# Two transformer blocks on one core: inputs turned by the host, weights in one array, and twelve idle matmuls at the start

## The chip, the core and the metric

The kernel runs on one core of one Trainium2 chip. The metric is device time in microseconds (us). Three runs of the kernel before gave 2495.00, 2495.05 and 2495.88 us; the median is 2495.05 us. The core's engines are called PE (TensorE, matrix products), ACT (ScalarE), DVE (VectorE), POOL (GpSimd) and SP (SyncE, which here only issues DMAs).

## The reference

256 tokens of 2048 features go through two blocks, all in float32. The first block has two layers; in each of them

```python
h = rmsnorm(x, norm_g[l])
proj = h @ w_in[l]                      # [256, 2048] @ [2048, 7168]
a_x, a_b, a_c, a_g, d_q, d_k, d_v, d_g, m_q, m_g = jnp.split(proj, offsets, axis=-1)
# a gated convolution over tokens (a_*), differential attention over the tokens (d_*)
mn = rmsnorm(mem, mem_norm_g[l])
mkv = mn @ w_mem_kv[l]                  # keys and values of 256 stored tokens, for the queries m_q
y = jnp.concatenate([y_a, y_d, y_m], axis=-1) @ w_out[l]
x = x + y
```

The second block projects again (`w_in_2`), runs two attention branches, merges them (`w_out_2`), attends to a second memory `mem_2` (normed, then `w_mem_kv_2`), and ends with a feed-forward part 2048 to 8192 to 2048 (`w_ff1_2`, `w_ff2_2`) and a last norm. A norm is `x * rsqrt(mean(x * x) + eps) * g`, over the features of one token. All weight matrices together are 440 MB and are used once.

## The kernel before

**Products.** Nearly all work is in `product`: 256 tokens times 512 columns of a weight matrix, over 16 feature tiles of 128. The activation lies "K-layout", features on the partitions, in tiles called A0h to A3h and B0h to B3h (high parts) and A0l to B3l (low parts), four feature tiles each, held in two slots "A" and "B"; the second index letter stands for high or low. Every float32 value is split into a part that the tensor engine's short format holds exactly (high) and the rest (low), and a product is three matmuls: high by high, high by low, low by high. The weights come in pieces of two feature tiles, 128 partitions by 1024 values (512 KB). For each piece SP issues a DMA into `raw` (L168, four buffers), ACT rounds it to `hi` (L169), DVE subtracts to get `lo` (L170, three buffers of hi and lo), and PE runs 12 matmuls (L187 hi by xh, L188 lo by xh, L189 hi by xl, for two feature tiles and two token tiles). In the listing's order `acc<-hi,A0h`, `hi` is the operand that streams through PE and `A0h` the one that is loaded into it. Eight pieces make a product.

**Work between the pieces.** After each piece `pump` runs one step of the background work (attention, the memory's preparation) and the delayed steps that are due; a scheduler then sets the order of the instructions on each engine under the limits that `issue_after` gives. Each engine runs its instructions in that order, so an ACT step that stands ahead of the next `hi` delays that `hi`.

**x and the memories.** Tensors arrive with tokens on the partitions. `first_input` loads x in four parts of 512 features in the first product, turns each by 8 transposes on PE (`to_klayout`, L156), and splits them from PSUM with the gains (L146 on ACT, L147 on DVE); ACT also squares the token-major x for the norm (L207). The gains are loaded by 18 small DMAs and turned by PE (L64, L392, L393). `memory_parts` does the same for `mem` in layer 0 and again in layer 1 (tile `mem_l`) and for `mem_2` (tile `mem_b`): four parts, each loaded, squared, turned by 8 transposes, split. A norm's factor 1/rms comes from `rsqrt`, some 17 small DVE steps (L85 to L87 are in it).

**The end.** The last product's weights (`last_weights`) are kept whole: pieces 0 to 3 in the tiles of slot A, pieces 4 to 7 in own tiles w4h to w7l, so that the two token tiles can be done one after the other (L966 to L968).

**Where tiles lie.** In a partition's memory the pools follow each other in the order in which they are opened: first the constants (`cst`), then slots A and B (`klp`), `raw` (`wrp`), `hi` and `lo` (`wsp`), and the rest; each tile takes a multiple of 32 bytes. In the built program the byte addresses are: A0h 39424, B0h 72192, `raw` from 104960, `hi` 121344, 125440 and 129536, `lo` from 133632, all of them multiples of 512; w4h is at 188096, w4l at 192192, and w4h to w7l are all 64 bytes past a multiple of 128. Of the attention's float32 tiles that stream through PE, `mv` is at 200384 (64 past a multiple of 128) and `pT` at 145920 and 147968 (multiples of 128).

Of the kernel before, what the change touches and what calls it, by code (L numbers as in the profile page):

```python
# [23 lines left out]
PSUM = bass.MemoryType.PSUM  # L24


@with_exitstack
def tile_two_blocks(
    ctx: ExitStack, tc: tile.TileContext,
    x, mem, norm_g, w_in, conv_w, conv_b, diff_q_norm_g, diff_k_norm_g, lambda_q1, lambda_k1,  # L30
    lambda_q2, lambda_k2, diff_head_norm_g, mem_norm_g, w_mem_kv, mem_q_norm_g, mem_k_norm_g,
    w_out, mem_2, positions_2, g_mix_2, w_in_2, g_cq_2, w_uq_2, w_iq_2, w_dsa_o_2, w_moba_o_2,
    w_out_2, g_mem_q_2, g_mem_kv_2, w_mem_q_2, w_mem_kv_2, w_mem_o_2, g_ff_2, w_ff1_2, w_ff2_2,
    g_final_2, out,
):
    nc = tc.nc
# [86 lines left out]
    class KLayout:  # L123
        """An activation with its features on the partitions, in two parts, in groups of four tiles."""
# [14 lines left out]
    def split(dst, src, gain=None):  # L139
        """dst = (hi, lo), each rounded to the tensor engine's short format; hi + lo = src * gain."""  # L140
# [8 lines left out]
    def to_klayout(kl, k0, nk, src, gain0=None):  # L149
        """Tiles k0.. of kl from src(t, j), [128 tokens, 128 features] each."""  # L150
# [14 lines left out]
    def weights(src, k0, nk, c0, n, hl=None):  # L165
        raw = wrp.tile([P, 2, 512], F32, name="raw", tag="raw")
        hi, lo = hl or [wsp.tile([P, 2, 512], F32R, name=a, tag=a) for a in ("hi", "lo")]
        nc.sync.dma_start(raw[:, 0:nk, 0:n], rows(src, k0 * P, nk * P, c0, n))  # L168
        A.activation(hi[:, 0:nk, 0:n], raw[:, 0:nk, 0:n], AF.Copy)  # L169
        V.tensor_tensor(lo[:, 0:nk, 0:n], raw[:, 0:nk, 0:n], hi[:, 0:nk, 0:n].bitcast(F32),  # L170
                        op=ALU.subtract)
# [181 lines left out]
    def first_input(i):  # L353
# [660 lines left out]
```

## Time and profile before

| | us |
|---|---|
| median of three runs | 2495.05 |
| the profiled execution, first to last instruction (span) | 2491.6 |
| median less span (the page gives no other time for the profiled execution) | 3.45 |
| PE busy | 2464.8 (99%) |
| DVE busy | 1423.0 (57%) |
| ACT busy | 1256.6 (50%) |
| PE idle between its instructions, all waits of the list by releaser | about 15 |

The span is the time from the first to the last instruction; what lies around it is the same launch work in every run and is not in the trace. PE's busy time counts a matmul from its start to a modelled end, so that neighbours overlap; the distance between the starts of two matmuls is what each costs. "Idle before" and the releaser behind "<-" tell what an engine waited for.

### The profile page before, as it was taken

To read this page: it belongs to the slowest core of one execution; us is meant where nothing else is said; L and a number is where in the kernel's file an instruction comes from. 1 tells how busy PE (TensorE), PEld (TensorE's weight loads), DVE (VectorE), ACT (ScalarE), POOL (GpSimd) and SP (SyncE) were. 2 spreads that over 40 slices of the span, in tenths; PEclk is the share of its full clock that TensorE was granted. 3 is DMA by queue.
4 is the path that set the end of the run, shared out by engine and by line. 5 is a ranking of instruction groups with operands and counts; after the bars stand their busy time and mean duration, and the time that the engine had idled before them with its cause. 6 is when DMAs were issued, how large, how long until landed. Compare 5 with 4: busy or idle time off the path is not lost.

```text
span 2491.6 us, 30607 instructions
## 1 busy us (share of the span) xinstructions
PE 2464.8 (99%) x11453; PEld 2035.2 (82%) x11453; DVE 1423.0 (57%) x2140; ACT 1256.6 (50%) x1808; POOL 3.3 (0%) x49
## 2 busy tenths in 40 slices
PE   8999999999999999999999999999999999999998
PEld 6888888888888888987888888888888888888876
DVE  6655566575556765555655545565645445445463
ACT  6554555465445554554554444565553443443452
POOL 0000000000000000000000000000000000000000
PEclk9999999999999999999999999999999999999999
DMA  6565555566655556654655566554665666666672
GB/s 229 183 186 165 173 162 183 185 206 187 180 168 167 170 182 177 192 171 136 195 174 163 173 190 194 179 192 156 184 186 193 188 190 192 190 187 194 186 243 87
DMA packets 234884, 450.76 MB, mean 181 GB/s; under 512 B 14260, under 2 KB 21104, under 8 KB 234608
## 3 DMA queue, kind: packets, MB, share of 16 engines
q1 hardware_dynamic: 234304, 446.72, 59.2%
q8 instruction: 90, 1.47, 0.2%
q10 hardware_dynamic: 432, 2.10, 0.2%
q14 instruction: 58, 0.48, 0.1%
HBM read 446.66 MB, written 2.10 MB: 180 GB/s over the span
## 4 chain that ended last, share of the span: by engine, by line
PE 95%; DMA 2%; ACT 2%; DVE 1%; issue 0%; SPq 0%; ACTq 0%; DVEq 0%
PE acc L187 29%; PE acc L189 29%; PE acc L188 29%; PE tr L156 2%; DMA mem_l<-in_mem_dram 1%; PE tr L294 1%; DMA raw<-in_w_ff_dram 1%; ACT hi L169 1%; PE sc L759 1%; PE sc L538 1%; DVE lo L170 0%; PE po L566 0%; PE sc L321 0%; PE sc L788 0%; PE tr L313 0%; ACT sq L207 0%
## 5 line engine op out<-in xcount | busy, mean ns | idle before, releaser
L170 DVE TENSOR_TENSOR lo<-raw,hi 128x1024 fp32r<-128x1024 f32 (+1 forms) x832 | 1010.8, 1215 | 916.4 <-ACT hi L169 914.8
L169 ACT ACTIVATE hi<-raw 128x1024 fp32r<-128x1024 f32 (+1 forms) x832 | 875.5, 1053 | 1050.1 <-PE acc L189 967.2
L187 PE MATMUL acc<-hi,A0h 128*128 128x512 f32 (+2 forms) x560 | 222.6, 398 | 2.0 <-ACT A0h L146 2.0
L187 PE MATMUL acc<-hi,A1h 128*128 128x512 f32 (+2 forms) x560 | 222.2, 397 | 0.6 <-ACT A1h L146 0.6
L187 PE MATMUL acc<-hi,A2h 128*128 128x512 f32 (+2 forms) x560 | 221.5, 396 | 0.6 <-ACT A2h L146 0.6
L187 PE MATMUL acc<-hi,A3h 128*128 128x512 f32 (+2 forms) x560 | 220.0, 393 | 0.1
L188 PE MATMUL acc<-lo,A0h 128*128 128x512 f32 (+2 forms) x560 | 218.5, 390 | 0.0
L189 PE MATMUL acc<-hi,A0l 128*128 128x512 f32 (+2 forms) x560 | 217.7, 389 | 0.0
L188 PE MATMUL acc<-lo,A1h 128*128 128x512 f32 (+2 forms) x560 | 217.1, 388 | 0.4 <-DVE lo L170 0.4
L188 PE MATMUL acc<-lo,A2h 128*128 128x512 f32 (+2 forms) x560 | 217.4, 388 | 0.0
L189 PE MATMUL acc<-hi,A1l 128*128 128x512 f32 (+2 forms) x560 | 217.0, 388 | 0.1
L189 PE MATMUL acc<-hi,A2l 128*128 128x512 f32 (+2 forms) x560 | 216.9, 388 | 0.1
L189 PE MATMUL acc<-hi,A3l 128*128 128x512 f32 (+2 forms) x560 | 216.9, 387 | 0.0
L188 PE MATMUL acc<-lo,A3h 128*128 128x512 f32 (+2 forms) x560 | 216.8, 387 | 0.0
L187 PEld LDWEIGHTS acc<-hi,A0h 128*128 128x128 f32 x560 | 105.7, 189 | 25.6 <-ACT A0h L146 3.1
L187 PEld LDWEIGHTS acc<-hi,A1h 128*128 128x128 f32 x560 | 105.2, 188 | 23.1 <-issue 2.7
L187 PEld LDWEIGHTS acc<-hi,A2h 128*128 128x128 f32 x560 | 105.2, 188 | 22.6 <-issue 1.7
L189 PEld LDWEIGHTS acc<-hi,A0l 128*128 128x128 f32 x560 | 105.5, 188 | 21.5 <-DVE A0l L147 0.4
L187 PEld LDWEIGHTS acc<-hi,A3h 128*128 128x128 f32 x560 | 105.2, 188 | 21.7 <-issue 1.3
L189 PEld LDWEIGHTS acc<-hi,A1l 128*128 128x128 f32 x560 | 105.0, 188 | 21.9 <-DVE A1l L147 0.5
L189 PEld LDWEIGHTS acc<-hi,A2l 128*128 128x128 f32 x560 | 105.0, 188 | 21.5 <-DVE A2l L147 0.5
L189 PEld LDWEIGHTS acc<-hi,A3l 128*128 128x128 f32 x560 | 105.1, 188 | 21.2
(414 smaller groups left out, 3682.2 us busy)
## 6 DMA issues: line engine op xcount, KB each, us to landing
raw<-in_w_in_dram SPq DMA_DIRECT2D x360, 512.0 KB
raw<-in_w_ff_dram SPq DMA_DIRECT2D x256, 512.0 KB
raw<-in_w_out_dram SPq DMA_DIRECT2D x96, 512.0 KB
raw<-in_w_mem_kv_dram SPq DMA_DIRECT2D x48, 512.0 KB
raw<-in_w_dsa_o_dram SPq DMA_DIRECT2D x16, 512.0 KB
raw<-in_w_moba_o_dram SPq DMA_DIRECT2D x16, 512.0 KB
raw<-in_w_in_dram SPq DMA_DIRECT2D x16, 384.0 KB
mem_l<-in_mem_dram SPq DMA_DIRECT2D x8, 512.0 KB
```

Of the source, the lines that this page charges most:

```text
L156: T.transpose(tr[:, j, t * P:(t + 1) * P], src(t, j0 + j), ident)
L169: A.activation(hi[:, 0:nk, 0:n], raw[:, 0:nk, 0:n], AF.Copy)
L170: V.tensor_tensor(lo[:, 0:nk, 0:n], raw[:, 0:nk, 0:n], hi[:, 0:nk, 0:n].bitcast(F32), op=ALU.subtract)
L187: T.matmul(o, xh[:, ts], hi[:, j, 0:n], start=first, stop=False)
L188: T.matmul(o, xh[:, ts], lo[:, j, 0:n], start=False, stop=False)
L189: newest[0] = T.matmul(o, xl[:, ts], hi[:, j, 0:n], start=False, stop=last).ins
L294: T.transpose(tr[:, j, t * P:(t + 1) * P], q[:, t, (j0 + j) * P:(j0 + j + 1) * P], ident)
L538: T.matmul(sc[c][:, t, :], qkT[hp, h, t * P:(t + 1) * P], qkT[hp, 6 + h, :], start=True, stop=True)
L759: T.matmul(ps[:, lo:lo + n], qiT[hp, j, t * P:(t + 1) * P], kiT[hp, 0:n], start=True, stop=True)
```

## The change

Four things are changed.

- The host hands over `x_t`, `mem_t` and `mem2_t` with features on the partitions and all gains as one array of 128 by 192, loaded by one DMA on ACT's queue. The transposes of x in the first product and of the memories are gone. The first product loads two feature tiles of x with each piece of weights (the first piece in halves); the memories come in four parts of four feature tiles, and the splits read them from SBUF instead of PSUM.
- The memories' norm factor is formed by `TStats`: squares on ACT, sums over feature tiles on DVE, and two PE matmuls of 128 by 1 with a column of ones (`tot`, L226) that add over the partitions. For `mem` it is formed in layer 0 and used in both layers.
- All weights lie in one array `stream` of 840 blocks in the order of use, each a contiguous 512 KB (rows of 4 KB for a partition instead of two of 2 KB).
- Twelve matmuls of the identity by itself stand first on PE. The token-major x is loaded in the second product, where its squares are taken too; the first product's output is normed in the second product's last pieces. In both layers the memory-query product (columns 6144 on) stands ahead of the two `w_mem_kv` products, and in layer 0 the memory's background work begins one product later.

```diff
+WARM = 12
...
-    st0 = scr.tile([32, P], F32, name="st0", tag="pT")
-    nc.sync.dma_start(st0, norm_g.rearrange("l (k p) -> (l k) p", p=P))
+    cols = cst.tile([P, 192], F32, name="cols")
+    A.dma_start(cols, gains)
...
+    ones = cst.tile([P, 1], F32, name="ones")
...
-    T.transpose(tr[:, 0:32], st0, ident[0:32, 0:32])
-    first_gains = V.tensor_copy(cols[:, 0:32], tr[:, 0:32])
+    for _ in range(WARM):
+        warmed = T.matmul(tr[:, 0:P], ident, ident, start=True, stop=True)
...
-        nc.sync.dma_start(raw[:, 0:nk, 0:n], rows(src, k0 * P, nk * P, c0, n))
+        for i in range(pieces):
+            ms = slice(i * m // pieces, (i + 1) * m // pieces)
+            nc.sync.dma_start(raw[:, ms], stream[len(plan), :, ms])
+            A.activation(hi[:, ms], raw[:, ms], AF.Copy)
+            V.tensor_tensor(lo[:, ms], raw[:, ms], hi[:, ms].bitcast(F32), op=ALU.subtract)
...
+    class TStats:
+        def __init__(self, name):
+            self.sum = None
+            self.r = cst.tile([P, 2], F32, name=f"r_{name}")
+            self.hr = cst.tile([P, 2], F32, name=f"hr_{name}")
+        def add(self, src):
+            sq = sq_tile().rearrange("p t n -> p (t n)")[:, 0:2 * S]
+            A.activation(sq, src.rearrange("p k s -> p (k s)"), AF.Square)
+            a, b = sq[:, 0:S], sq[:, S:2 * S]
...
+                V.tensor_tensor(self.sum, self.sum, a, op=ALU.add)
+                V.tensor_tensor(self.sum, self.sum, b, op=ALU.add)
+        def done(self, d=D):
+            tot = trp.tile([P, 512], F32, name="tot", tag="tr")
+            for t in range(2):
+                T.matmul(tot[:, t:t + 1], self.sum[:, t * P:(t + 1) * P], ones, start=True, stop=True)
+            rsqrt(self.r, tot[:, 0:2], 2, 1.0 / d)
...
         for c in range(4):
-            part = scr.tile([P, 2, 512], F32, name=f"mem_{name}", tag="tok")
-            nc.sync.dma_start(part, rows(src[0], 0, S, c * 512, 512))
-            yield
-            for t in range(2):
-                stats.add(t, c, part[:, t, :])
-            to_klayout(kl, 4 * c, 4, lambda t, j: part[:, t, j * P:(j + 1) * P], gain0 + 4 * c)
-            yield
+            part = scr.tile([P, 4, S], F32, name=f"mem_{name}", tag="tok")
+            nc.sync.dma_start(part, src[:, 4 * c:4 * c + 4, :])
+            yield
+            for j in (0, 2):
+                if stats is not None:
+                    stats.add(part[:, j:j + 2, :])
+                for i in (j, j + 1):
+                    split(kl(4 * c + i), part[:, i, :], col(gain0 + 4 * c + i))
+                yield
...
     def first_input(i):
-        if i % 4:
-            return
-        cs = slice(i * P, i * P + 512)
-        nc.sync.dma_start(x_sb[:, :, cs], rows(x[0], 0, S, i * P, 512))
-        to_klayout(kl, i, 4, lambda t, j: x_sb[:, t, (i + j) * P:(i + j + 1) * P], C_NORM + i)
-        with tc.issue_after(newest[1]):
-            for t in range(2):
-                r_x.add(t, i // 4, x_sb[:, t, cs])
+        if i % 4 == 0:
+            part[0] = scr.tile([P, 4, S], F32, name="x_part", tag="tok")
+        a = part[0]
+        for k in ((0, 1), (1, 2)) if i == 0 else ((i, i + 2),):
+            nc.sync.dma_start(a[:, k[0] % 4:(k[1] - 1) % 4 + 1, :], x_t[:, k[0]:k[1], :])
+        for k in (i, i + 1):
+            split(kl(k), a[:, k % 4, :], col(C_NORM + k))
...
-        r_m = Stats(f"m{l}")
+    r_m = TStats("m")
...
+        def first_stats(i):
+            if i % 2 == 0 and i < 8:
+                cs = slice(256 * i, 256 * i + 512)
+                nc.sync.dma_start(x_sb[:, :, cs], x[:, :, cs])
+                for t in range(2):
+                    r_x.add(t, i // 2, x_sb[:, t, cs])
+            elif i == 10:
+                r_x.done()
+            elif i == 12:
+                queries_keys(0, first_acc)
...
+        background.append(memory_parts(f"l{l}", mem_t, ml, C_MEM + 16 * l, None if l else r_m))
```

The lists that follow show the instructions of an engine in their order, without times: line, operation, tiles, shape, and how many alike follow each other. First PE from the start of the program, before.

```order
L64 MATMUL tr<-ident,st_83 128x32
L156 MATMUL tr<-ident,x_sb 128x128 x8
L187 MATMUL acc<-hi,A0h 128x512
L188 MATMUL acc<-lo,A0h 128x512
L187 MATMUL acc<-hi,A0h 128x512
L189 MATMUL acc<-hi,A0l 128x512
```

The same place after the change (L192 to L194 are the three matmuls of a product now).

```order
L64 MATMUL tr<-ident 128x128 x12
L192 MATMUL acc<-hi,A0h 128x512
L193 MATMUL acc<-lo,A0h 128x512
L194 MATMUL acc<-hi,A0l 128x512
L192 MATMUL acc<-hi,A0h 128x512
```

The gains' transpose and the 8 transposes of x are gone from the head of the queue, and the idle matmuls stand there. Next the DMAs that SP issues from the start, before (`st` is a tile of gains).

```order
L56 DMA st_83<-in_norm_g_dram 32x128
L358 DMA x_sb<-in_x_dram 128x2x512
L168 DMA raw<-in_w_in_dram 128x2x512 x2
L358 DMA x_sb<-in_x_dram 128x2x512
L168 DMA raw<-in_w_in_dram 128x2x512 x2
```

After the change (`x_part` is x with features on the partitions).

```order
L401 DMA x_part<-in_x_t_dram 128x256 x2
L171 DMA raw<-in_stream_dram 128x512 x2
L401 DMA x_part<-in_x_t_dram 128x512
L171 DMA raw<-in_stream_dram 128x1024
L401 DMA x_part<-in_x_t_dram 128x512
L171 DMA raw<-in_stream_dram 128x1024
```

The first matmul needs two transfers of 128 KB of x and the first 256 KB of weights now, where it needed 16 KB of gains, 512 KB of x and 512 KB of weights. Last, ACT at the densest part of the layer-0 memory's preparation, before: in the third product (B2h, B3h: the memory's tiles; qk: a product's output).

```order
L169 ACTIVATE hi<-raw 128x1024
L146 ACTIVATE B2h<-tr,cols 128x256
L277 ACTIVATE qk<-acc,r_x_98 128x512
L207 ACTIVATE sq,ss_m_468<-mem_l_717 128x512
L146 ACTIVATE B3h<-tr,cols 128x256
L207 ACTIVATE sq,ss_m_468<-mem_l_717 128x512
L146 ACTIVATE B3h<-tr,cols 128x256 x2
L277 ACTIVATE qk<-acc,r_x_98 128x512
L146 ACTIVATE B3h<-tr,cols 128x256
L278 ACTIVATE sq<-qk 128x1024
L169 ACTIVATE hi<-raw 128x1024 x6
```

After the change, in the memory-query product.

```order
L172 ACTIVATE hi<-raw 128x1024 x2
L214 ACTIVATE sq<-mem_l_743 128x512
L145 ACTIVATE B1h<-mem_l_743,cols 128x256 x4
L145 ACTIVATE B2h<-mem_l_829,cols 128x256
L214 ACTIVATE sq<-mem_l_743 128x512
L145 ACTIVATE B2h<-mem_l_829,cols 128x256 x2
L318 ACTIVATE qk<-acc,r_x_109 128x512
L145 ACTIVATE B2h<-mem_l_829,cols 128x256
L214 ACTIVATE sq<-mem_l_829 128x512
L318 ACTIVATE qk<-acc,r_x_109 128x512
L172 ACTIVATE hi<-raw 128x1024
```

Ten steps stood between one `hi` and the next, and thirteen stand there now; the block of splits has come together, since no transpose on PE stands ahead of each of them any more.

The constants change too: `ones` adds 32 bytes to `cst`, and one `r`, `hr` pair of the memory less takes 64 away. In the built program after the change A0h is at 39392, B0h at 72160, `raw` from 104928, `hi` at 121312, 125408 and 129504, `lo` from 133600, w4h at 188064: slots, weights and the tiles behind them lie 32 bytes lower than before.

## Rows read from the trace of the kernel before

**Rows 1.** The page's first part (busy time, share of the span, instructions) and its summary of the chain of work that ended last, by engine.
```profile
PE 2464.8 (99%) x11453; PEld 2035.2 (82%) x11453; DVE 1423.0 (57%) x2140; ACT 1256.6 (50%) x1808; POOL 3.3 (0%) x49
...
PE 95%; DMA 2%; ACT 2%; DVE 1%; issue 0%; SPq 0%; ACTq 0%; DVEq 0%
```
**Rows 2.** What PE waited for in the whole span: us in total, times, longest.
```profile
PE tr L156 <- DMA x_sb<-in_x_dram: 3.0, 1, 3.0
PE tr L64 <- POOL u L628: 2.5, 1, 2.5
PE acc L188 <- DVE lo L170: 2.2, 4, 0.8
PE acc L187 <- ACT A0h L146: 2.0, 1, 2.0
PE tr L156 <- DMA mem_l<-in_mem_dram: 1.6, 3, 0.9
PE acc L187 <- ACT hi L169: 1.2, 1, 1.2
PE tr L156 <- DVE rs_w L85: 0.8, 1, 0.8
...
PE tr L294 <- DVE B1l L147: 0.3, 1, 0.3
```
**Rows 3.** PE in order of time from the start: start, duration, matmul, count, and the idle time before it with its releaser.
```profile
2.52 0.28 PE L64 MATMUL tr<-ident,st 32*128 32x32 f32 x1 [2.52 <-POOL u L628]
5.83 1.97 PE L156 MATMUL tr<-ident,x_sb 128*128 128x128 f32 x8 [3.03 <-DMA x_sb<-in_x_dram]
9.85 0.79 PE L187 MATMUL acc<-hi,A0h 128*128 128x512 f32 x1 [2.05 <-ACT A0h L146]
...
13.27 0.63 PE L188 MATMUL acc<-lo,A0h 128*128 128x512 f32 x1
13.70 0.63 PE L187 MATMUL acc<-hi,A0h 128*128 128x512 f32 x1
...
14.95 0.39 PE L187 MATMUL acc<-hi,A0h 128*128 128x512 f32 x1
15.18 0.39 PE L188 MATMUL acc<-lo,A0h 128*128 128x512 f32 x1
...
39.96 0.27 PE L393 MATMUL tr<-ident,st 64*128 64x64 f32 x1
40.16 0.50 PE L187 MATMUL acc<-hi,A0h 128*128 128x512 f32 x1
```
**Rows 4.** Stretches of one us: length, busy time of PE, PEld, DVE, ACT, POOL with counts, granted clock, DMA share, GB/s.
```profile
1.00:2.00 1.00, 0.00 (x0) 0.00 (x0) 0.00 (x0) 1.00 (x1) 0.97 (x18) 1.00 0.05 13
2.00:3.00 1.00, 0.28 (x1) 0.17 (x1) 0.67 (x3) 0.21 (x2) 0.51 (x6) 1.00 0.78 88
3.00:4.00 1.00, 0.00 (x0) 0.00 (x0) 0.03 (x1) 0.00 (x0) 0.00 (x0) 1.00 0.89 244
4.00:5.00 1.00, 0.00 (x0) 0.00 (x0) 0.00 (x0) 0.00 (x0) 0.00 (x0) 1.00 0.92 277
5.00:6.00 1.00, 0.17 (x1) 0.17 (x2) 0.00 (x0) 0.00 (x0) 0.00 (x0) 1.00 1.00 360
6.00:7.00 1.00, 1.00 (x6) 1.00 (x7) 0.00 (x0) 0.00 (x0) 0.00 (x0) 1.00 0.98 348
7.00:8.00 1.00, 0.80 (x4) 0.40 (x2) 0.00 (x0) 0.92 (x1) 0.00 (x0) 1.00 1.04 401
8.00:9.00 1.00, 0.00 (x0) 0.00 (x0) 0.83 (x1) 0.77 (x2) 0.00 (x0) 1.00 1.05 408
```
**Rows 5.** ACT and DVE in the first product, by group: tiles, shape, count, busy us, mean ns of one, idle before.
```profile
L170 DVE TENSOR_TENSOR lo<-raw,hi 128x1024 fp32r<-128x1024 f32 x10 | 12.2, 1224 | 14.8 <-ACT hi L169 14.7
L169 ACT ACTIVATE hi<-raw 128x1024 fp32r<-128x1024 f32 x10 | 10.6, 1056 | 10.3 <-DMA raw<-in_w_in_dram 6.1 <-PE acc L189 4.1
L207 ACT ACTIVATE sq<-x_sb 128x512 f32<-128x512 f32 x8 | 5.0, 625 | 0.1
...
L146 ACT ACTIVATE A1h<-tr,cols 128x256 fp32r<-128x256 f32 x4 | 1.7, 467 | 1.0 <-DVE A1l L147 1.0
```
**Rows 6.** From the chain that ended last, in order of time: start and length of the links (96 product matmuls lie between the two).
```profile
1970.85 0.87 PE tr L156 x8
1993.50 0.87 PE tr L156 x8
```
**Rows 7.** PE in order of time in the last product: the end of the pieces in slot A's tiles, the pieces in w4h to w7l, and the second token tile's beginning.
```profile
2458.95 0.39 PE L966 MATMUL acc<-A0h,B0h 128*128 128x512 f32 x1
...
2464.39 0.39 PE L966 MATMUL acc<-w4h,B2h 128*128 128x512 f32 x1
...
2469.99 0.39 PE L966 MATMUL acc<-A0h,B0h 128*128 128x512 f32 x1
```
**Rows 8.** Stretches in the feed-forward part, columns as in Rows 4.
```profile
2380.00:2416.00 36.00, 33.02 (x146) 26.19 (x145) 22.95 (x21) 22.48 (x24) 0.00 (x0) 1.00 0.79 254
2404.00:2408.00 4.00, 2.83 (x12) 1.99 (x12) 1.23 (x2) 1.16 (x2) 0.00 (x0) 1.00 0.90 289
```
**Rows 9.** Two groups of float32 matmuls of the attention with one shape: the streaming tile is `mv` in the first, `pT` in the second; busy us, mean ns of one, idle before.
```profile
L344 PE MATMUL po<-mv,pT 128*128 128x128 f32 x64 | 8.4, 274 | 0.0
...
L813 PE MATMUL po<-pT,va 128*128 128x128 f32 x16 | 3.1, 274 | 0.0
```

More of the change, by code (lines that the diff above doesn't have):

```diff
@@ L24 @@
 PSUM = bass.MemoryType.PSUM
+WARM = 12
+BLOCKS = 840
+WARM = 12
 @with_exitstack
 def tile_two_blocks(
[L29 to L34, printed above, removed]
+    ctx: ExitStack, tc: tile.TileContext, plan, stream, x, x_t, mem_t, mem2_t, gains, lambda_q1, lambda_k1,
+    lambda_q2, lambda_k2, positions_2, g_final_2, out,
 ):
@@ L179, in product @@
                 ahead(i)
-            hi, lo = weights(src, ks[i] - kw0, 2, c0, n)
+            hi, lo = weights(src, [k - kw0 for k in ks[i:i + 2]], c0, n,
+                             pieces=2 if not plan else 1)
             for j in range(2):
@@ L186, in product @@
                     o = acc[t][:, 0:n]
-                    T.matmul(o, xh[:, ts], hi[:, j, 0:n], start=first, stop=False)
-                    T.matmul(o, xh[:, ts], lo[:, j, 0:n], start=False, stop=False)
-                    newest[0] = T.matmul(o, xl[:, ts], hi[:, j, 0:n], start=False, stop=last).ins
+                    T.matmul(o, xh[:, ts], hi[:, ns], start=first, stop=False)
+                    T.matmul(o, xh[:, ts], lo[:, ns], start=False, stop=False)
+                    newest[0] = T.matmul(o, xl[:, ts], hi[:, ns], start=False, stop=last).ins
             pump()
@@ L196, in sq_tile, with at, half @@
         return scr.tile([P, 2, 512], F32, name="sq", tag="sq", bufs=1)
+    class TStats:
[7 more added lines that the diff above has]
+            a, b = sq[:, 0:S], sq[:, S:2 * S]
+            if self.sum is None:
+                self.sum = tny.tile([P, S], F32, name="ssq", tag="ssq", bufs=2)
+                V.tensor_tensor(self.sum, a, b, op=ALU.add)
+            else:
+                V.tensor_tensor(self.sum, self.sum, a, op=ALU.add)
[5 more added lines that the diff above has]
+            rsqrt(self.r, tot[:, 0:2], 2, 1.0 / d)
+            V.tensor_scalar(self.hr, self.r, 0.5, None, op0=ALU.mult)
+        def at(self, t):
+            return self.r[:, t:t + 1]
+        def half(self, t):
+            return self.hr[:, t:t + 1]
     class Stats:
@@ L464, in tile_two_blocks, with queries_keys @@
     slopes = [2.0 ** (-8.0 * (h + 1) / 6) for h in range(6)]
+    r_m = TStats("m")
     def first_layer(l, kl, r_x, p1):
-        w = w_in[l]
+        w = ("w_in", l)
         qkT = p1.tile([P, 12, S], F32, name="qkT", tag="qkT")
         y = KLayout("B")
-        r_m = Stats(f"m{l}")
-        for i in range(3):
-            ps = first_acc if (l, i) == (0, 0) else product(w, 3072 + 512 * i, 512, kl, ALL)
+        def queries_keys(i, ps):
             q = normed_heads(ps, 512, 64, r_x, "qk")
@@ L489, in first_layer @@
         mv = p1.tile([P, 2, 512], F32, name="mv", tag="mv")
-        drain()
-        ps = product(w_mem_kv[l], 0, 512, ml, ALL)
-        qm = normed_heads(ps, 512, P, r_m, "mk")
-        later(5, lambda q=qm: heads_to(mkT, 0, q, 4))
-        ps = product(w_mem_kv[l], 512, 512, ml, ALL)
-        for t in range(2):
-            A.activation(mv[:, t, :], ps[t], AF.Copy, scale=r_m.at(t))
         ps = product(w, 6144, 512, kl, ALL)
@@ L499, in first_layer @@
         later(5, lambda q=qm: heads_to(mqT, 0, q, 4, prods[:, 2 + l:3 + l]))
+        drain()
+        ps = product(("w_mem_kv", l), 0, 512, ml, ALL)
+        qm = normed_heads(ps, 512, P, r_m, "mk")
+        later(5, lambda q=qm: heads_to(mkT, 0, q, 4))
+        ps = product(("w_mem_kv", l), 512, 512, ml, ALL)
+        for t in range(2):
+            A.activation(mv[:, t, :], ps[t], AF.Copy, scale=r_m.at(t))
         mg = p1.tile([P, 2, 512], F32, name="mg", tag="mg")
@@ L817, in tile_two_blocks @@
     for i in range(2):
-        ps = product(w_uq_2[0], 512 * i, 512, cql, list(range(4)))
+        ps = product(("w_uq_2", 0), 512 * i, 512, cql, list(range(4)))
         roped_heads(ps, 0, 4, r_c, qaT, 4 * i)
@@ L848, in tile_two_blocks @@
             pump()
-        py = product(w_dsa_o_2[0], 512 * c, 512, yk, list(range(8)))
+        py = product(("w_dsa_o_2", 0), 512 * c, 512, yk, list(range(8)))
         th = sq_tile()
@@ L902, in tile_two_blocks @@
         background.append(two_heads(h))
-    ps = product(w_mem_kv_2[0], 512, 512, mem_l, ALL)
+    ps = product(("w_mem_kv_2", 0), 512, 512, mem_l, ALL)
     for t in range(2):
```

154 lines of the change are left out of this document (75 added, 79 removed).

## The prediction

> **What bounds the kernel now.** Read the page's first part and its chain first: PE is busy 99% of the span and makes 95% of the chain that ended last [rows 1]. The reader is to see that nothing but PE's own work, and the few places where PE waits, can move the time; ACT and DVE have half their time free. PE's waits come second: 15 us in all, of which 7.5 lie before the first product's second piece (3.0, 2.5 and 2.0), 3.1 at the memories (mem_l 1.6, rs_w 0.8, B1l 0.3, and 0.4 of the lo waits, which lies in the 40 to 80 us stretch) and 3.0 in the feed-forward part (1.2 for hi, 1.8 of lo) [rows 2]. Third, what a product costs where nothing waits: from 1970.85 + 0.87 to 1993.50 are 21.78 us for 96 matmuls, 0.2269 each, 2.72 for a piece; eight transposes cost 0.87 [rows 6]. Fourth, the start, where those figures don't hold yet: the first 96 product matmuls take from 9.85 to 39.96, with some gains turned among them [rows 3].
>
> The profiled execution has a span of 2491.6; the median is 3.45 above it. I subtract from the span and add the 3.45 back, so the sum applies to 2495.05 alike.
>
> **A. The start.** Before, the second product begins at 40.16 [rows 3]. Now 622 KB must land for the first matmul's piece (gains 98, two x tiles 262, half a piece 262). Summing rows 4 up from 13 KB moved before 2 us: 345 KB by 4, 622 by 5, 1731 by 8, 2139 by 9. The second piece of before (1552 KB, reached at 7.6) let ACT start at 8.37, so landing lags the sum by some 0.9. The first x transfer is now SP's first issue, 0.45 earlier, so 622 KB are there at about 5.5. Half a hi and half a lo (1.06 and 1.22 for a whole [rows 5]) put the first matmul at 6.0 and its lo at 6.6. The second piece needs 1670 KB: landed 8.35, hi 9.4, lo 10.6. PE waits there, and then has 83 matmuls at 0.227, 18.8 us: end 29.4, or 30.4 if a later piece is as tight. I take 29.9: **10.3 gained**, 6.5 to 11.5 by whether data come 1 to 2 us later. Later pieces bring 786 KB, 1.9 us at the 408 GB/s of [rows 4], against 2.72 of matmuls; ACT has 1.06 + 2 x 0.47 and DVE 1.22 + 2 x 0.48 (estimated as ACT's) per piece, below 2.72 too.
>
> The twelve idle matmuls lie in the time before 5.5. Eight cold transposes of the same shape took 1.97 [rows 3], so twelve take 3.0, from 2.5 to 5.5: hidden, at most 0.3 sticks out. The row shows PE at half rate when its work begins: product matmuls start 0.43 apart at 13.27, which is the 1.2 GHz level, and 0.23 apart from 14.95, the 2.4 GHz level, although the granted-clock column says 1.00 from 2 us on [rows 3, 4]. PE had worked from 5.83 and paused for 2.05 in between. The Trainium skill ("TensorE: Matmul & The Clock Gate", Part 1) says that the array starts at half its clock, is released by sustained activity, and that the moment differs from run to run; the spacing agrees, the granted column does not. That rule would let the idle matmuls miss their purpose, and is the first rival's ground.
>
> The token-major x now comes in the second product: 2 MB more in its first four pieces, 1 MB per 2.72 us, 386 GB/s, below the 401 to 408 of rows 4 and covered by four raw buffers. I cost it at nothing; without that cover it would be 1 to 5 us. Its squares (8 x 0.63 on ACT [rows 5]) lie beside matmuls.
>
> **B. The memories' transposes.** 3 x 32 = 96 on PE's path, 12 times 0.87 [rows 6]: **10.4 gained**. Above and below that is nothing: PE does nothing else in that time, and no product's matmul is behind anything but PE itself.
>
> **C. Waits in the memory stretches.** The 3.1 us above go, as no transpose waits for a load. What comes late instead is `hi`: the burst on ACT between two of them was 5 splits, two copies, two squares and a wide square, some 2.4 + 1.3 + 1.6 + 1.2 = 6.5 us, and cost PE 0.4; the new one has 8 splits, three squares, two copies, 3.7 + 1.9 + 1.3 = 6.9 (copies taken like squares [rows 5]). Three hi buffers cover 5.4 to 8.2, so some 0.8 is lost. For mem_2, DVE gets 16 adds of about 0.4 (estimated from its 1.22 for four times the size); 0.7. Net **1.6**, between -3.8 (two pieces of 2.7 lost) and +3.1. The first query product's norm factor is formed at the second product's piece 5 and used at piece 6: ACT may wait there, as it waits for DVE's factor before, and `hi` behind it has 2.7 us or more of cover.
>
> **D. Feed-forward waits.** 3.0 us are lost where the DMA engines are 0.79 to 0.90 busy [rows 8] and last_weights adds pieces. Blocks with rows of 4 KB may help there; no row shows such a transfer. Bounds -1 (issue order worsens) and +3 (all goes); I take **+1.0**, as the nearest row, the first product's, ran at 408 rather than 289 GB/s.
>
> **E. The new norm's matmuls.** Four of 128 x 1, with everything of the next piece queued behind them on PE, and they wait for DVE's last sum. Their inputs come a piece ahead of them, so **-0.3**, at worst -3 (a piece). Two buffers for rsqrt's steps instead of four cost nothing, as DVE runs these steps one after the other anyway.
>
> Sum 10.3 + 10.4 + 1.6 + 1.0 - 0.3 = 23.0: span 2468.6, time **2472.0**.
>
> **Rivals.**
>
> *The clock comes up late.* The idle matmuls end, PE pauses about 0.5, and the first piece still runs at 0.43: 12 x 0.43 = 5.2, to 11.2, then 7 more until 14.3, then 77 x 0.227: end 31.8, loss 1.9; with data 2 us late, 4: 2474 to 2476. For it: PE needed 8.5 us of mixed work before [rows 3]. Against: it paused 2.05 then.
>
> *The memory stretches starve hi.* If the thirteen steps on ACT are served ahead of two hi and not one, a piece (2.7) is lost in layer 0, and the same on DVE at mem_2, with 5 to 10 us in all: 2477 to 2482. For it: ACT's order, shown above. Against: the like burst cost 0.4.
>
> *Every product matmul slows down, since the tiles moved by 32 bytes.* Slower. In the last product, 24 matmuls that stream from slot A take 2464.39 - 2458.95 = 5.44, 0.2267 each; the next 24, from w4h to w7l, take 5.60, 0.2333 each, and no transfer or wait lies there [rows 7]. What sets these tiles apart is their place, 64 bytes past a multiple of 128 (and above 188 KB). After the change every hi, lo and slot tile lies 96 past. 840 pieces x 12 = 10080 matmuls at +0.0067 are 67 us: 2472 + 67 = **2539**. No row shows 96: with a price in proportion it is 0.0100, 101 us, 2573; at half, 2505. It decides as soon as the spacing exceeds 0.229. Against: the price could belong to the address range, not the offset; and float32 matmuls that stream `mv` (64 past) take the 274 ns of those that stream `pT` (0 past) [rows 9], though these take twice as long per column and may hide it. The Trainium skill ("SBUF — State Buffer", Specifications) counts in lines of 16 bytes and charges for crossing to a new one; 32 bytes change no such crossing, so by that rule the time stays at 2472. It doesn't explain the 0.2333 either.
>
> *The new array does nothing.* Transposes and idle time go but the loads of the first product and of mem in 4 KB rows come later than before by as much: 2490 to 2500. Against: the first piece needs 622 KB now and needed 1040 (16 of gains, 512 of x, 512 of weights).
>
> **How the numbers follow.** The forecast with its small variants (2465 to 2478, the late clock's 0.08 beside it) has 0.40; starved hi 0.07; slowed matmuls 0.40 (0.06 at half price, 0.20 at 0.0067, 0.14 above); nothing gained 0.03; transfers that bound throughout 0.02. The likeliest single case is 2472; its own range is 2465 to 2481. Since cases of both signs hold most of the chance, the range must reach to the slowed matmuls at 0.0067: 2465 to 2545, which leaves out 0.14 + 0.02 above and little below. A difference of 0.2% (5 us) is what a measurement of this kernel can tell. Faster 0.40 + 0.08 + 0.07 = 0.55, within 0.2% 0.03, slower 0.42.
>
> **What would show it.** The start: second product's first matmul near 29.9, first product matmul near 6.0, matmuls 0.23 apart by the second piece. Memories: no L156 on mem tiles, ACT's burst followed by a hi wait under 1 us. The spacing in an undisturbed product: 0.2267 or 0.233 to 0.237; this one number separates 2472 from 2539. I'm wrong if the product's 96 matmuls no longer take 21.8 us, or if PE's waits at the memories exceed 5 us.

## The result and the profile after

The changed kernel takes 2477.01 us (median of four runs, 2476.38 to 2478.88); the kernel before, run beside it, 2495.47. The ratio is 0.9929, with a 95% interval of 0.9917 to 0.9941: about 18 us faster, where 23 were forecast. The forecast of 2472.0 is 5.0 us too low; the measured time lies in the likeliest case's own range, 2465 to 2481.

PE is still the bound. The page's first part answers to [rows 1], and the waits of PE to [rows 2].

```profile
PE 2453.6 (99%) x11354; PEld 2027.8 (82%) x11354; DVE 1432.8 (58%) x2150; ACT 1249.8 (50%) x1777; POOL 3.3 (0%) x50
```

```profile
PE acc L193 <- DVE lo L173: 6.1, 8, 2.2
PE acc L192 <- ACT hi L172: 3.3, 3, 1.8
PE tr L64 <- POOL u L666: 2.5, 1, 2.5
PE tot L226 <- DVE ssq L221: 0.7, 1, 0.7
```

The waits for x and mem are gone, and in their place PE waits 9.4 us for the split weights, `hi` and `lo`, where it waited 3.4 before. Where that happens shows in PE's order of time, which answers to [rows 3].

```profile
2.46 4.67 PE L64 MATMUL tr<-ident 128*128 128x128 f32 x24 [2.46 <-POOL u L666]
6.89 0.47 PE L192 MATMUL acc<-hi,A0h 128*128 128x512 f32 x1
...
11.47 0.49 PE L192 MATMUL acc<-hi,A0h 128*128 128x512 f32 x1 [0.94 <-ACT hi L172]
12.73 0.64 PE L193 MATMUL acc<-lo,A0h 128*128 128x512 f32 x1 [0.76 <-DVE lo L173]
13.17 0.63 PE L194 MATMUL acc<-hi,A0l 128*128 128x512 f32 x1
...
23.53 0.50 PE L193 MATMUL acc<-lo,A2h 128*128 128x512 f32 x1 [0.69 <-DVE lo L173]
...
31.44 0.50 PE L193 MATMUL acc<-lo,A3h 128*128 128x512 f32 x1 [2.18 <-DVE lo L173]
...
37.40 0.39 PE L192 MATMUL acc<-hi,A0h 128*128 128x512 f32 x1
```

The twelve idle matmuls (two records each) last until 6.89. The first product then runs at the 2.4 GHz level (matmuls 0.23 apart), waits at 10.4 to 12.7, and falls back to the 1.2 GHz level: eight matmuls from 12.73 start 0.43 apart. This time the granted clock shows it too (the column behind POOL's):

```profile
12.00:13.00 1.00, 0.27 (x1) 0.27 (x2) 1.00 (x3) 0.92 (x2) 0.00 (x0) 0.97 0.90 264
13.00:14.00 1.00, 1.00 (x3) 0.74 (x3) 1.00 (x4) 1.00 (x3) 0.00 (x0) 0.50 1.01 358
```

The second product begins at 37.40. It began at 40.16, so the start gave 2.8 us.

**How the span stands to the time.** In all runs of either kernel the measured time is 1.8 us above the span (2478.88 beside 2477.1; 2495.53 beside 2493.7). The execution of before that the profile shows, with 2491.6, thus took about 2493.4, less than any of the four runs beside it (2495.00 to 2495.96), and that of after is the slowest of its four. The two traces are 14.5 us apart, the medians 18.5. The stages below are told from the two traces:

| stretch, from the starts of product matmuls | before | after | gained |
|---|---|---|---|
| start to the first product's first matmul | 9.85 | 6.89 | 2.96 |
| the first product | 30.31 | 30.51 | -0.20 |
| layer 0 up to the memory gates, where the order of products differs | 141.94 | 140.13 | 1.81 |
| layer 1's memory stretch | 54.91 | 51.05 | 3.86 |
| mem_2's stretch | 50.71 | 46.75 | 3.96 |
| end of the feed-forward part, before the last token tiles | 93.09 | 92.09 | 1.00 |
| all the rest | | | 1.1 |

### The profile page after: what moved, and what is told of

It reads as the page before. It is cut to its first block, busy times and chain, and to the rows that moved or that the text cites. A ratio compares the mean times of both kernels' runs of the same rounds, so it can differ in the third digit from the quotient of the medians.

```text
span 2477.1 us, 30382 instructions
## 1 busy us (share of the span) xinstructions
PE 2453.6 (99%) x11354; PEld 2027.8 (82%) x11354; DVE 1432.8 (58%) x2150; ACT 1249.8 (50%) x1777; POOL 3.3 (0%) x50
## 4 chain that ended last, share of the span: by engine, by line
PE 95%; DMA 2%; DVE 1%; ACT 1%; issue 0%; SPq 0%; ACTq 0%; DVEq 0%
PE acc L192 29%; PE acc L193 29%; PE acc L194 29%; PE tr L155 1%; DMA raw<-in_stream_dram 1%; PE tr L335 1%; PE sc L797 1%; DVE lo L173 1%; PE sc L576 1%; PE po L604 0%; PE sc L362 0%; PE tr L354 0%; PE sc L826 0%; ACT hi L172 0%; DMA x_sb<-in_x_dram 0%
## 5 line engine op out<-in xcount | busy, mean ns | idle before, releaser
L173 DVE TENSOR_TENSOR lo<-raw,hi 128x1024 fp32r<-128x1024 f32 (+3 forms) x833 | 1010.8, 1214 | 885.8 <-ACT hi L172 883.8
L172 ACT ACTIVATE hi<-raw 128x1024 fp32r<-128x1024 f32 (+3 forms) x833 | 875.3, 1051 | 1033.1 <-PE acc L194 957.1
L192 PE MATMUL acc<-hi,A0h 128*128 128x512 f32 (+2 forms) x560 | 222.3, 397 | 2.8 <-ACT hi L172 2.8
L192 PE MATMUL acc<-hi,A1h 128*128 128x512 f32 (+2 forms) x560 | 222.1, 397 | 0.0
L192 PE MATMUL acc<-hi,A2h 128*128 128x512 f32 (+2 forms) x560 | 221.2, 395 | 0.0
L192 PE MATMUL acc<-hi,A3h 128*128 128x512 f32 (+2 forms) x560 | 219.6, 392 | 0.0
L194 PE MATMUL acc<-hi,A0l 128*128 128x512 f32 (+2 forms) x560 | 218.5, 390 | 0.0
L194 PE MATMUL acc<-hi,A2l 128*128 128x512 f32 (+2 forms) x560 | 217.0, 388 | 0.0
L194 PE MATMUL acc<-hi,A1l 128*128 128x512 f32 (+2 forms) x560 | 217.0, 387 | 0.0
L194 PE MATMUL acc<-hi,A3l 128*128 128x512 f32 (+2 forms) x560 | 216.7, 387 | 0.0
L192 PEld LDWEIGHTS acc<-hi,A0h 128*128 128x128 f32 x560 | 105.7, 189 | 26.4 <-ACT hi L172 3.9
L193 PEld LDWEIGHTS acc<-lo,A0h 128*128 128x128 f32 x560 | 106.1, 190 | 22.5 <-DVE lo L173 2.6
L193 PEld LDWEIGHTS acc<-lo,A3h 128*128 128x128 f32 x560 | 105.3, 188 | 23.4 <-DVE lo L173 3.3
L194 PEld LDWEIGHTS acc<-hi,A0l 128*128 128x128 f32 x560 | 105.9, 189 | 21.2
L192 PEld LDWEIGHTS acc<-hi,A1h 128*128 128x128 f32 x560 | 105.2, 188 | 21.9 <-issue 2.6
L192 PEld LDWEIGHTS acc<-hi,A2h 128*128 128x128 f32 x560 | 105.3, 188 | 21.5 <-issue 1.7
L192 PEld LDWEIGHTS acc<-hi,A3h 128*128 128x128 f32 x560 | 105.2, 188 | 21.5 <-issue 1.3
L193 PEld LDWEIGHTS acc<-lo,A2h 128*128 128x128 f32 x560 | 105.3, 188 | 21.3 <-DVE lo L173 1.4
```

Of the source, the lines that this page charges most:

```text
L172: A.activation(hi[:, ms], raw[:, ms], AF.Copy)
L173: V.tensor_tensor(lo[:, ms], raw[:, ms], hi[:, ms].bitcast(F32), op=ALU.subtract)
L192: T.matmul(o, xh[:, ts], hi[:, ns], start=first, stop=False)
L193: T.matmul(o, xh[:, ts], lo[:, ns], start=False, stop=False)
L194: newest[0] = T.matmul(o, xl[:, ts], hi[:, ns], start=False, stop=last).ins
```

## The experiments

Twelve kernels were run, all variants of the changed kernel, four runs each but for e5. For each the table gives the second product's first matmul, the length of the memory-query product of layer 0 (27.53 in the changed kernel) and of the feed-forward end, from its trace; then the median and the ratio to the kernel before that ran on the same chip, with its 95% interval.

Two things limit what the table can tell. The traced execution is one of the runs, and not always a typical one: the slowest of the four in the changed kernel and e4, the fastest in e1, e6, e8, e9, e10 and e11. And the changed kernel, e2, e5, e8 and e13 have the same order on PE, ACT and DVE in the first product, yet their second products begin anywhere from 36.43 to 37.75. So differences of about 1.3 us in that column, and medians whose intervals overlap widely, show nothing.

| kernel | second product | query product | end | median | ratio |
|---|---|---|---|---|---|
| changed | 37.40 | 27.53 | 92.09 | 2477.01 | 0.9929 [0.9917, 0.9941] |
| e1, one idle matmul | 31.63 | 25.87 | 90.21 | 2473.49 | 0.9909 [0.9895, 0.9924] |
| e2, buffers for x | 36.86 | 27.81 | 90.65 | 2477.23 | 0.9926 [0.9909, 0.9942] |
| e3, lambdas late | 33.33 | 25.48 | 90.95 | 2474.41 | 0.9915 [0.9900, 0.9930] |
| e4, three edits of the start | 34.97 | 28.24 | 92.89 | 2476.74 | 0.9928 [0.9913, 0.9943] |
| e5, offset 64 | 37.75 | 27.35 | 91.71 | 2478.72 | one run |
| e6, small loads early | 38.06 | 25.67 | 91.12 | 2480.30 | 0.9943 [0.9927, 0.9960] |
| e8, fine steps | 36.43 | 22.67 | 90.33 | 2474.14 | 0.9918 [0.9903, 0.9933] |
| e9, one idle, fine steps | 31.38 | 23.68 | 90.53 | 2469.78 | 0.9900 [0.9885, 0.9914] |
| e10, order | 35.94 | 25.45 | 90.50 | 2477.71 | 0.9932 [0.9917, 0.9947] |
| e11, order, fine steps | 35.67 | 23.10 | 89.78 | 2471.99 | 0.9915 [0.9898, 0.9931] |
| e12, six idle, fine steps | 35.56 | 22.65 | 90.10 | 2470.68 | 0.9908 [0.9893, 0.9923] |
| e13, rows of 2 KB | 37.12 | 27.70 | 89.75 | 2477.51 | 0.9933 [0.9918, 0.9948] |

### The place of the tiles (e5)

```diff
+    pad = cst.tile([P, 24], F32, name="pad")
+    V.memset(pad, 0.0)
```

> 96 bytes of unused constants shift all slots, hi, lo and the tiles behind them from 96 to 64 past a multiple of 128, where w4h to w7l lay before; w4h itself comes to a multiple of 128. Rival of the forecast (the offset sets the 0.2333): all product matmuls 0.2333 apart and those from w4h to w7l 0.2267, time near 2477 + 67 = 2544. Theory (the place above 188 KB sets it, or something else of these tiles): spacing 0.2267 everywhere but 0.2333 in w4h to w7l as before, time 2475 to 2480.

The last product, in order of time: of the changed kernel (tiles 96 past a multiple of 128, w4h 32 past), then of e5 (64 past, w4h 0 past). They answer to [rows 7].

```profile
2444.96 0.39 PE L1004 MATMUL acc<-A0h,B0h 128*128 128x512 f32 x1
...
2450.40 0.39 PE L1004 MATMUL acc<-w4h,B2h 128*128 128x512 f32 x1
...
2456.00 0.39 PE L1004 MATMUL acc<-A0h,B0h 128*128 128x512 f32 x1
```

```profile
2444.81 0.39 PE L1006 MATMUL acc<-A0h,B0h 128*128 128x512 f32 x1
...
2450.25 0.39 PE L1006 MATMUL acc<-w4h,B2h 128*128 128x512 f32 x1
...
2455.85 0.39 PE L1006 MATMUL acc<-A0h,B0h 128*128 128x512 f32 x1
```

Both give 5.44 for 24 matmuls from slot A (0.2267) and 5.60 from w4h to w7l (0.2333). Over the three kernels slot A's tiles have been tried at 0, 96 and 64, those of w at 64, 32 and 0: the offset has no effect, and the 0.2333 stays with the w tiles. The single run of e5 is enough for this, as the spacing is read from its trace. The slower rival falls. Whether their height (above 188 KB) or something else makes the 16 cycles of 2.4 GHz was not tried.

### The start (e1, e2, e3, e4, e6)

```diff
-WARM = 12
+WARM = 1
```

> One idle matmul at the start instead of twelve, all else as in the changed kernel. Theory (the idle matmuls bring the clock up and pay, though the starved start hides much of it): the first product's first piece runs with matmuls 0.43 us apart, the second product starts 0.5 to 3 us later than the 37.4 us of the changed kernel, time 2477.5 to 2480. Rival (they only keep PE busy until 6.9 us while data are there at 6.0, and the waits for pieces 2 and 3 decide): first product matmul near 6.1 us, second product at 36.5 to 37.5, time 2476 to 2477.

Neither held: with one idle matmul the second product starts 5.8 us earlier, and the time falls by 3.5. PE in order of time of e1:

```profile
2.46 0.80 PE L64 MATMUL tr<-ident 128*128 128x128 f32 x2 [2.46 <-POOL u L666]
6.11 0.80 PE L192 MATMUL acc<-hi,A0h 128*128 128x512 f32 x1 [2.86 <-ACT hi L172]
...
11.27 0.61 PE L194 MATMUL acc<-hi,A0l 128*128 128x512 f32 x1
11.69 0.42 PE L192 MATMUL acc<-hi,A0h 128*128 128x512 f32 x1
...
29.00 0.50 PE L193 MATMUL acc<-lo,A3h 128*128 128x512 f32 x1 [0.54 <-DVE lo L173]
```

The first product runs at half rate until 11.7 (the granted-clock column reads 1.00 there, as in the kernel before), and little is lost by it: its third piece begins at 14.47, and at 14.07 to 14.90 in seven kernels with twelve idle matmuls (e2, e3, e4, e5, e8, e10 and e11). These run faster, but PE waits 0.3 to 0.8 us in them for the second piece's `hi` or `lo`; in the changed kernel, whose clock falls there, the third piece begins at 16.95. From 11.7 on e1's first product has one wait, of 0.54, and no matmul at half rate; the changed kernel has its largest, of 2.18, there.

Where the 2.18 come from shows on DVE in the changed kernel, where the lambdas' loads (64 KB each, the same 512 bytes for every partition) stand behind the first product's last piece; the second group says how long such a load takes (KB each, us from issue to landing).

```profile
28.96 0.29 DVE L462 TENSOR_TENSOR lprod<-lamv 128x128 f32<-128x128 f32 x1 [1.84 <-DMA lamv<-in_lambda_k_dram]
...
30.17 1.22 DVE L173 TENSOR_TENSOR lo<-raw,hi 128x1024 fp32r<-128x1024 f32 x1
```

```profile
lamv<-in_lambda_k_dram SPq DMA_DIRECT2D x2, 64.0 KB, 6.6
```

DVE waits for the lambdas with the seventh piece's `lo` queued behind. In e1 the scheduler puts that `lo` ahead of the lambdas, so only the eighth piece waits. The number of idle matmuls thus also changes the order in which the scheduler lays out DVE and ACT.

```diff
-    lamv = scr.tile([P, 4, 2, 64], F32, name="lamv", tag="pT")
...
+        if l == 0:
+            lambdas()
```

> The four small loads of the lambdas and the steps that use them stand after the third product instead of after the first, all else as in the changed kernel. Theory (DVE waits for these loads with lo queued behind it, and PE waits 2.2 us for that lo at 31.4): the 2.2 us go, second product 2 to 3.5 us earlier, time 2473.5 to 2475. Rival (the positions' load, which stays and feeds DVE as well, takes the same place): a wait of 1 to 2 us on lo stays before 35 us and the time is 2475.5 to 2477.

The theory held: 33.33, 4.1 us earlier and so a little more than it said, the largest wait 0.77, the time 2.6 us less. In the trace layer 1's memory stretch takes 52.75 for 51.05. That is no loss that the edit is shown to cause: PE, ACT and DVE work in the same order there, and the traces with this order (the changed kernel, e1 to e6, e10 and e13) range from 50.89 to 52.75.

```diff
-            part[0] = scr.tile([P, 4, S], F32, name="x_part", tag="tok")
+            part[0] = klp.tile([P, 4, S], F32, name="x_part", tag=f"B{i // 4}h")
```

> The four parts of the feature-major x go to four own buffers (the idle slot B) instead of two, all else as in the changed kernel. Theory (SP stops at 6.5 us for the first part's buffer, and weights queue behind it; PE's waits at 11.5, 12.7 and 23.5 us and the fallen clock come from that): SP issues on without the gap to 10.5, these waits shrink to under 1 us together, the matmuls from 12.7 to 16.2 are 0.23 apart and not 0.43, the second product starts near 33 to 35 us instead of 37.4, time 2472 to 2475. Rival (the transfers themselves, not the order of issue, bound the start): waits move but do not shrink, second product within 1 us of 37.4, time 2476 to 2478.

The rival's numbers came. The seventh piece's first matmul comes 2.0 us earlier (26.84), but then PE waits 2.65 for its `lo`, which stands behind the lambdas, and seven matmuls start 0.43 apart. So the second product is only 0.5 us earlier, and the time the same. What takes the gain back is thus not the transfers, as the rival had it, but again the order on DVE.

```diff
+    A.dma_start(pos_i, positions_2.rearrange("o (t p) -> p (o t)", p=P))
...
+            part[0] = klp.tile([P, 4, S], F32, name="x_part", tag=f"B{i // 4}h")
...
+        if l == 0:
+            lambdas()
```

> Four buffers for x, the lambdas after the third product, and the positions loaded on ACT's queue at the start. Theory (these three are the whole of the lost start): second product starts near 31 us, where the forecast had 29.9, time 2470 to 2472. Rival (something else, the rate of transfers or the clock, keeps 3 us or more): second product at 33.5 or later, time 2473 to 2475.

The rival held for the start: 34.97, with seven waits of 0.2 to 0.8 for `hi` and `lo` before it and no large one. The time, 2476.74, is above its range; nothing is gained in all. Where two of the waits for `hi` (0.66 at 18.33, 0.55 at 28.34) come from shows on ACT.

```profile
16.61 0.32 ACT L447 ACTIVATE cos<-turn,halfpi 128x32 f32<-128x32 f32 x1 [1.32 <-DVE sin L453]
...
17.23 1.04 ACT L175 ACTIVATE hi<-raw 128x1024 fp32r<-128x1024 f32 x1
...
26.61 0.63 ACT L248 ACTIVATE sq<-x_sb 128x512 f32<-128x512 f32 x1 [4.43 <-DMA x_sb<-in_x_dram]
...
27.24 1.04 ACT L175 ACTIVATE hi<-raw 128x1024 fp32r<-128x1024 f32 x1
```

With the lambdas away, other steps stand ahead of the weights' split: ACT waits for a step on the positions with the fourth piece's `hi` behind it, and 4.43 for the token-major x with the seventh's.

```diff
+        if i == 4:
+            small_loads()
```

> The lambdas' and the positions' loads are issued by ACT in the first product's third piece instead of by SP behind the last; all else as in the changed kernel. Theory (DVE waits for these loads with lo behind it): no lo wait over 1 us between 28 and 36 us, second product near 33.3 us as with the lambdas put off, and no loss in layer 1 for it; time 2473 to 2475. Rival (256 KB of small rows early delay the pieces by as much): lo and hi waits of 1 us more before 20 us, second product after 36, time 2476 to 2479.

The rival's losses came, and more than it said: the third piece begins at 18.53 instead of near 14.5, the second product at 38.06, and the time is 2480.30. The reason is not shown to be the rival's, that 256 KB early delay the pieces' transfers. The scheduler put the first lambda step on DVE ahead of the second piece's `lo`:

```profile
12.17 0.29 DVE L465 TENSOR_TENSOR lprod<-lamv 128x128 f32<-128x128 f32 x1 [2.58 <-DMA lamv<-in_lambda_k_dram]
...
13.05 1.22 DVE L173 TENSOR_TENSOR lo<-raw,hi 128x1024 fp32r<-128x1024 f32 x1
```

DVE waits 2.58 for the load, PE then 2.76 for that `lo`, and eight matmuls start 0.43 apart: the wait that the edit was to remove came back earlier. What the loads cost the pieces' transfers beside that was not separated.

### ACT's order in the first product (e10, e11, e12)

```diff
+            last_hi[0] = A.activation(hi[:, ms], raw[:, ms], AF.Copy).ins
...
+        with tc.issue_after(last_hi[0] or warmed.ins):
+            for k in (i, i + 1):
+                split(kl(k), a[:, k % 4, :], col(C_NORM + k))
```

> Twelve idle matmuls as in the changed kernel, but in the first product ACT may split the next piece's x only after the hi of the piece before it; all else the same. Theory (it is the scheduler's order on ACT, three splits of x ahead of the fourth piece's hi, that starves the first product with twelve idle matmuls): the third piece pair begins near 20 us as with one idle matmul, the second product near 33 to 35 us, of which 2 are the lambdas' wait, time 2473.5 to 2476. Rival (the early clock itself runs PE into waits that the transfers set): second product at 36 to 38, time 2476 to 2479.

Half of it held: the fifth piece begins at 20.14, as in e1 (19.91), where the four kernels with the changed kernel's order and buffers (itself, e5, e8, e13) have 21.56 to 22.45, so the order on ACT did cost some 2 us. But then PE waits 3.02 for the seventh piece's `lo`, which stands behind the lambdas, PE falls to half rate, and the second product is at 35.94. The time, 2477.71, is in the rival's range and did not change beyond its interval.

> The same order in the first product, and the memory's preparation in fine steps. Theory (the two losses are separate and add): the kernel of e10 less 3 us, 2470.5 to 2473. Rival (fine steps gain only where the start is late, as transfers then run ahead): within 1 us of e10.

The theory held, 2471.99 against 2477.71. What a pause can cost beyond itself shows here best, on PE and in the granted clock:

```profile
28.75 0.50 PE L194 MATMUL acc<-lo,A3h 128*128 128x512 f32 x1 [3.05 <-DVE lo L174]
29.44 0.63 PE L193 MATMUL acc<-hi,A3h 128*128 128x512 f32 x1
...
32.00 0.63 PE L193 MATMUL acc<-hi,A3h 128*128 128x512 f32 x1
32.43 0.46 PE L194 MATMUL acc<-lo,A3h 128*128 128x512 f32 x1
```

```profile
28.00:29.00 1.00, 0.25 (x1) 0.25 (x2) 1.00 (x2) 0.59 (x2) 0.00 (x0) 1.00 1.06 412
29.00:30.00 1.00, 1.00 (x4) 0.76 (x4) 1.00 (x7) 0.97 (x5) 0.00 (x0) 0.58 1.00 406
30.00:31.00 1.00, 1.00 (x4) 0.81 (x3) 1.00 (x6) 0.83 (x1) 0.00 (x0) 0.50 1.05 410
```

After 3.05 us of waiting the matmuls from 29.44 to 32.43 start 0.43 apart, seven of them, 7 x 0.20 = 1.4 us on top.

Set beside e9 (one idle matmul and fine steps, below), e11 tells what the idle matmuls themselves are worth. The seventh piece begins at 25.31 here:

```profile
25.31 0.39 PE L193 MATMUL acc<-hi,A3h 128*128 128x512 f32 x1
```

and in e9 at the same time:

```profile
25.26 0.39 PE L192 MATMUL acc<-hi,A3h 128*128 128x512 f32 x1
```

So once ACT's order starves PE no more, twelve idle matmuls neither gain nor cost against one up to there. The second products are 4.3 us apart (35.67 and 31.38) because PE waits 3.05 in e11, with the half rate behind it, and 0.39 in e9, where the scheduler put the seventh `lo` ahead of the lambdas.

```diff
-WARM = 12
+WARM = 6
```

> Six idle matmuls, which leave the splits of x in pairs by themselves, and fine steps. Theory (the order decides, and an earlier clock is worth 1 to 2 us once it is right): second product at 30 to 31.5, time 2468.5 to 2470. Rival (six bring the clock up no sooner than one, or PE waits and the clock falls again): second product at 32 to 37, time 2470.5 to 2475.

The rival held for the start (35.56, with 2.11 for the lambdas and half rate behind it); the time is 2470.68 all the same, with the fine steps of the next part in it.

### The memory's preparation (e8, e9)

```diff
                 for i in (j, j + 1):
                     split(kl(4 * c + i), part[:, i, :], col(gain0 + 4 * c + i))
-                yield
+                    yield
```

> The memory's preparation yields after every split instead of after every second one; all else as in the changed kernel. Theory (the thirteen ACT steps between two hi in the memory-query product starve PE, and the pause halves the clock): no hi wait in that product, its 96 matmuls and the queries' transposes take near 23.1 us instead of 27.5, time 2473 to 2474.5. Rival (ACT waits for the memory's load with hi behind it, however the steps are cut): a hi wait of over 1 us stays, time 2476 to 2478.

The theory held for the product, 22.67 instead of 27.53, and there is no `hi` wait in it; the product after it takes 0.8 more (23.43 for 22.67). The time, 2474.14, is near the upper end of what it gave. In the changed kernel the burst on ACT reads:

```profile
80.60 0.63 ACT L214 ACTIVATE sq<-mem_l 128x512 f32<-128x512 f32 x1 [1.60 <-DMA mem_l<-in_mem_t_dram]
...
86.52 1.04 ACT L172 ACTIVATE hi<-raw 128x1024 fp32r<-128x1024 f32 x1
```

and PE behind it:

```profile
87.62 0.90 PE L192 MATMUL acc<-hi,A0h 128*128 128x512 f32 x2 [1.82 <-ACT hi L172]
88.88 0.80 PE L193 MATMUL acc<-lo,A0h 128*128 128x512 f32 x1 [0.36 <-DVE lo L173]
```

ACT waits 1.6 for the memory's load, then works 5.9 us through the thirteen steps before the next `hi`; PE waits 1.82 and 0.36 and runs at half rate until 91.5. With fine steps at most five of the memory's steps stand together in that product. ACT still waits for a load of the memory there with `hi` behind it, 2.96 at 91.62 in e8, and PE doesn't wait: such a wait alone need not cost PE anything. In the changed kernel wait and burst come together.

> One idle matmul instead of twelve, and the memory's preparation in fine steps. Theory (both losses add): e1's 2473.5 less the 2 to 3 us that e1 still lost in the memory-query product, 2470 to 2472. Rival (the gain of e1 was the chance of its launches, or fine steps only move the loss into the drain before the memory's product): 2473 to 2476.

The theory held: 2469.78, a little below its range and the lowest median, 0.9900 of the kernel before (e12's interval and e9's overlap). Both edits add. Fine steps gain in each of three pairs: 2.9 (e8 against the changed kernel), 3.7 (e9 against e1) and 5.7 (e11 against e10).

### The rows of the weights (e13)

```diff
-    stream = nc.dram_tensor("in_stream_dram", (BLOCKS, P, 1024), ...)
+    stream = nc.dram_tensor("in_stream_dram", (BLOCKS, 2, P, 512), ...)
```

> The one weight array as in the changed kernel, but each block stored as two halves with rows of 2 KB, as the weights' rows were before. Theory (longer rows let transfers run faster where they are late, at the end of the feed-forward part and in the start): the last 11 groups of four feature tiles take 87.5 us as before instead of 85 to 86.7, and the time is 1 to 3 us above the changed kernel, 2478 to 2480. Rival (row length is worth nothing): within 1 us, 2476 to 2478.

The rival held: 2477.51, and the end of the feed-forward part is even the shortest of all, 89.75. Rows of 4 KB instead of 2 KB are worth nothing here that the runs could tell (each kernel's four spread over 2.5 to 3.2 us). What shortens that end by 0.2 to 3.3 us in all kernels with the one array, against 93.09 in the single trace of before, stays open.

## Why the prediction was right or wrong, point by point

**The sign and the place: right.** The transposes' 10.4 us were on PE's path and are gone; the three memory stretches gain 9.6 in the traces, which is B's 10.4 less 0.8, where the forecast had 11.7 (B, C and E). Of the signs that it named, the undisturbed product's 21.8 us stayed (21.76); the second product at 29.9 (37.40), the first matmul at 6.0 (6.89) and a `hi` wait under 1 us at the memories (1.82) did not come.

**A, the start: wrong, 2.8 instead of 10.3 in the traces.** Three parts of the step failed. "The twelve idle matmuls lie in the time before 5.5" did not hold: they take 4.4 and not 3.0, and last to 6.89, 0.9 past the forecast's first matmul. "PE waits there, and then has 83 matmuls at 0.227" assumed that the second piece is the last one that is late. In fact SP stops in its order for a buffer of x or of weights, ACT in its order for x, DVE in its order for the lambdas, which were not in the working at all; after those at 10.4 and 12.7 three more waits follow, of 0.69, 2.18 and 0.32, and none of these was priced. The late clock as a rival came true in another form: after the idle matmuls the first product ran at 2.4 GHz, and the clock fell at the pauses of 0.94 and 0.76. With one idle matmul the kernel is 3.5 us faster (e1), but by the order that the scheduler then chose: e11 beside e9 shows that up to the seventh piece the idle matmuls themselves gave nothing and cost nothing.

**B: right** in size, as far as the layers show it (3.86 for layer 1, where no squares are left and a wait of 0.35 is gone too, against 3.48 for 32 transposes).

**C: wrong, about nothing instead of 1.6, and part of the starved-hi rival.** The 9.6 are B's 10.4 less 0.7 for E and less 0.1. "Some 0.8 is lost" for the burst on ACT: PE waits 2.2 there and loses another microsecond at half rate. e8 takes 4.9 us off that product. The burst itself was priced high enough, 6.9 against 5.9 measured; the step left out that ACT first waits 1.6 for the load, with burst and `hi` behind.

**D: right by chance.** 1.0 as taken, but e13 shows no gain from longer rows, the reason given, and the traces after the change alone vary from 89.75 to 92.89 there.

**E:** 0.7 for PE's wait at `tot` against 0.3 taken.

**The 3.45 us around the span: mis-sized.** They are 1.8; the profiled execution was no median one. In the traces the gain misses the forecast's 23.0 by 8.5: 7.5 in A, 2.1 in B, C and E together, less 1.1 gained elsewhere that was not forecast. In the medians it misses by 4.5 only, since the traced execution of before lies below its median and that of after above.

**The range: right by its width.** 2465 to 2545 says little, and 2477.01 is also the edge of the starved-hi rival (2477 to 2482), so only the traces tell the cases apart. The rival of the slowed matmuls, which held 0.40 of the chance, rested on one true row and a wrong reading of it; it made the range wide; the changed kernel's spacing of 0.2267 and e5 show that the offset plays no part.

## What to carry to other kernels

When a stage at the start gets shorter, the next thing to look up is what each in-order queue still waits for there, small loads of constants first: here a 64 KB load held the weights' split behind it on DVE, and when it was moved (e4, e6), another step or the same one held it elsewhere. Idle matmuls gave nothing here: PE at the full rate waited for data until it was no further than PE at half rate (third piece at 14.43 in e11, at 14.38 in e9). Changing their number moves a scheduler's whole order, so they are to be tried in several numbers, one among them. A background step that was broken up by a PE transpose before each part becomes one burst when the transposes go; it has to be cut anew.

## What the runs showed that was not expected

- A pause of PE (0.94 and 0.76 with one matmul between in the changed kernel, 2.11 in e12, 2.65 in e2, 3.05 in e11) is followed, at once or a few matmuls later, by seven or eight matmuls at the 1.2 GHz level. Not each pause is: behind the 2.18 in the changed kernel and the 0.84 and 0.76 in e12 the matmuls start 0.23 apart. The length of the pause alone doesn't decide it, and what does stays open.
- Kernels differ in how far their runs spread: e10's four lie from 2474.3 to 2479.9, e9's from 2468.9 to 2470.1. Whether such pauses make the spread isn't shown; e8, with no matmul at half rate in its trace behind the start, spreads over 4.9.
- Matmuls that stream from w4h to w7l start 0.2333 apart and not 0.2267, at offsets 64, 32 and 0 alike.
